# GLA's neighbour level as one more level in the burst of small products

## The chip, the cores and the metric

The kernel runs on one core of a Trainium2 chip. The metric is the device time of one execution in microseconds. Before the change it is 1476.96 us, the median of three runs between 1476.38 and 1477.36 us.

The engines are called as the profile calls them: PE is TensorE, DVE is VectorE, ACT is ScalarE, POOL is GpSimd, SP is SyncE, which here issues nearly all DMAs.

## The reference: what is computed

One layer of a hybrid decoder runs over 1024 prompt tokens and 8 single sample tokens of width 1024. Two branches share one input projection: gated linear attention (GLA, 4 heads, key width 128, value width 256) and RWKV-7 (16 heads of 64). A sigmoid gate merges them, then come the output projection and a layer norm. The change touches only GLA's attention inside a chunk. For one head it is, in the reference:

```python
b = jnp.cumsum(gi, axis=2)
diff = b[:, :, :, None, :] - b[:, :, None, :, :]
decay = jnp.exp(jnp.where(mask, diff, -jnp.inf))
A = jnp.einsum('bhid,bhjd,bhijd->bhij', qi, ki, decay)
o = jnp.einsum('bhij,bhjv->bhiv', A, vi) + jnp.einsum('bhid,bhdv->bhiv', qi * jnp.exp(b), S)
```

`A[i, j]` is the product of query i and key j over the 128 key dimensions, each dimension decayed by its own factors between token j and token i. All values are float32.

## The kernel before, in words

**Passes and blocks.** The 1024 tokens are done in two passes of 512 (the first with the 8 samples beside it). `blocks` sends the input projection through PE in blocks of 128 output columns; every product is done in three parts with operands split into a high and a low share (`wpart`, `xs`), accumulated in the PSUM banks `proj`. ACT and DVE move the results into row buffers (`row`, 33 of them). When the rows of a GLA head or of an RWKV pair are there, its own chain of work is started (`gla_head`, `pair`). After the second pass's projections come the up projections of both branches and the output projection, which are almost nothing but wide products on PE.

**What sets the order.** Each piece of work is a Python generator, a stream, that yields one operation after the other. `Order.run` is a list scheduler: it looks at the next operation of every stream, reckons with a table of costs (`price`) when it could start, subtracts the stream's priority, and writes down the earliest. Operations named `E` may go to DVE or POOL, those named `C` to ACT or DVE, whichever would end first by the reckoning. The result is one fixed order of instructions for each engine. A change in any stream therefore shifts the order of all of them. `together` makes one operation of a list of products, so that they stand on PE without anything between them.

**The GLA head.** It runs eight times: four heads, two passes, one after the other (`headed`). A head works on rows of 128 key dimensions (partitions) by 512 tokens: `qp_` holds the queries, `km_` the keys, `al` the decay of each token. Two chunks of 128 tokens are interleaved in a row (`paired`), the second backwards in time. The matrix A of a chunk is built by levels m = 1, 2, 4, ... 64 (`LEVELS`). At level m a chunk is cut into blocks of 2m tokens; the level gives the products of the queries of one half of each block with the keys of the other half. After each level the keys and queries of the halves are multiplied in place by the decay over their half (`E.tensor_mul(y, y, ...)`, two products and a small third for the next level's decays), so that plain products give decayed ones.

The levels are done in four ways before the change:

- *The diagonal* (token with itself, `d0`). DVE or POOL multiplies keys and queries element by element into a row (`u`), DVE transposes it in blocks of 32x32 (`STREAM_TRANSPOSE`), sums each block's rows (`TENSOR_REDUCE`, into the tile `pair`), and adds the four groups of 32 partitions with small sums. A masked copy (`copy_predicated`, mask `lev`) puts the sums on the diagonal of `AC`, a tile that holds the 32x32 blocks on A's diagonal.
- *Level 1*, the neighbours (`d1`), in the same way: a second element-by-element product, a second transpose and reduction, the second half of the same small sums, and a second masked copy, beside the diagonal. Only then come the decay products of level 1.
- *Levels 2 to 16* (`small`). For each, two copies on ACT or DVE put the level's keys and queries (128x256 each) side by side into a row (`kept`). At level 32 one `together`, the burst, multiplies 32 keys with 32 queries for each of the eight diagonal blocks and each level, into one PSUM bank `pl`; masked copies take from each result the places of its level into `AC`.
- *Level 32* goes in the same burst straight from the keys and queries; *level 64* has products of its own.

The rows `kept` of the four levels are the two spare rows `z` and `vk1` and two more that are fetched for it. The burst is `big<-row 128x32` in the profile: 5 x 8 products, each of which stands there as two records.

All operations go through one helper (L217), so the groups of the profile are told apart by their tiles and shapes.

## Time and profile before

| what | value |
|---|---|
| median of three runs | 1476.96 us |
| the profiled execution | 1478.35 us |
| its span, first to last instruction | 1476.5 us |
| mean granted clock of PE | 0.998 |
| busy: PE, DVE, ACT, POOL | 1446.6, 1163.0, 878.9, 108.8 us |
| HBM traffic over the span | 214 GB/s |

The profile's groups give busy time, the mean length of one in ns, and the idle time of the engine before them with what ended it. Matmuls are pipelined and their ends are modelled, so PE's busy share is not a share of its peak. Waits give the engine that waited, what ended the wait, and then the total, the number and the longest. In the chain, each step is followed back to what released it.

### The profile page before, as it was taken

The page shows a single profiled execution, that of the slowest core. Times are in us where ns is not written, and L with a number is a line of the kernel's source. Part 1 is how long each engine was busy: PE and PEld are TensorE (multiplying, and loading weights), DVE is VectorE, ACT ScalarE, POOL GpSimd, SP SyncE. Part 2 cuts the span into 40 slices and gives each one's busy share as a digit, 9 for nine tenths or more (in the row PEclk, how much of TensorE's full clock was granted, in tenths as well). Part 3 has the DMA queues.
Part 4 walks back from the last instruction along what each step waited for, and adds up shares of the span by engine and source line. Part 5 has one row for each costly group of instructions (what it writes and reads, how often), then busy time and mean ns, then how long its engine had stood idle before and what let it go on. Part 6 is the DMA issues. An engine that isn't in the chain of part 4 may idle for free.

```text
span 1476.5 us, 31483 instructions
## 1 busy us (share of the span) xinstructions
PE 1446.6 (98%) x11158; PEld 1258.8 (85%) x11158; DVE 1163.0 (79%) x3071; ACT 878.9 (60%) x2302; POOL 108.8 (7%) x205
## 2 busy tenths in 40 slices
PE   9999999999999999999999999999999999999997
PEld 6999989999999998787878777778787899988786
DVE  6697879987899777967998898888876876755665
ACT  5666767775776677655775564465546746643210
POOL 1001010100110001000110210020000000000000
PEclk9999999999999999999999999999999999999999
DMA  8877887669765878548646457656654768987432
GB/s 308 278 260 228 260 268 239 215 212 313 259 240 193 289 259 269 174 140 249 207 131 198 148 160 240 205 153 172 182 172 142 246 196 253 295 300 258 135 109 84
DMA packets 211258, 318.96 MB, mean 216 GB/s; under 512 B 91811, under 2 KB 107180, under 8 KB 211100
## 3 DMA queue, kind: packets, MB, share of 16 engines
q1 hardware_dynamic: 211100, 316.93, 67.1%
q8 instruction: 89, 1.46, 0.4%
q14 instruction: 69, 0.57, 0.1%
HBM read 197.19 MB, written 118.61 MB: 214 GB/s over the span
## 4 chain that ended last, share of the span: by engine, by line
PE 77%; DVE 14%; ACT 3%; DMA 2%; issue 2%; SPq 1%; POOL 0%; POOLq 0%; DVEq 0%; ACTq 0%
PE proj L217 48%; PE big L217 20%; DVE row L217 6%; PE pch L217 5%; PE pY L217 4%; ACT row L217 2%; DVE X L217 1%; DVE wide L217 1%; DVE Xt L217 1%; SPq L217 1%; DVE pair L217 1%; ACT L401 1%; DVE az L217 1%; DVE bk L217 1%; DVE ac L217 1%
## 5 line engine op out<-in xcount | busy, mean ns | idle before, releaser
L217 PE MATMUL proj<-xs,wpart 128*128 128x264 f32 (+2 forms) x5640 | 1022.8, 327 | 1.0 <-DVE row L217 0.8
L217 PEld LDWEIGHTS proj<-xs,wpart 128*128 128x128 f32 x5640 | 811.2, 189 | 82.1 <-issue 10.3
L217 DVE TENSOR_TENSOR row<-row 128x512 f32<-128x512 f32 (+8 forms) x327 | 173.1, 537 | 13.0 <-ACT row L217 6.6
L217 ACT CAST wpart<-wraw 128x512 fp32r<-128x512 f32 x210 | 129.6, 622 | 89.7 <-PE proj L217 36.3
L217 DVE TENSOR_TENSOR wpart<-wraw,wpart 128x512 fp32r<-128x512 f32 x198 | 137.2, 695 | 34.4 <-ACT wpart L217 32.0
L217 ACT ACTIVATE row<-row 128x512 f32<-128x512 f32 (+3 forms) x197 | 117.6, 606 | 13.0 <-DVE row L217 4.1
L217 PE MATMUL big<-xs,wpart 128*128 128x512 f32 (+2 forms) x576 | 102.9, 332 | 0.8 <-DVE xs L217 0.7
L217 DVE TENSOR_TENSOR Xt<-X,wide 128x60 f32<-128x60 f32 (+21 forms) x432 | 94.7, 219 | 9.4
L217 ACT ACTIVATE row<-proj,omu 128x256 f32<-128x256 f32 (+1 forms) x99 | 54.0, 546 | 77.7 <-PE proj L217 77.2
L217 POOL TENSOR_TENSOR row<-row 128x512 f32<-128x512 f32 (+7 forms) x58 | 60.2, 1043 | 536.7 <-DVE row L217 190.5
L217 DVE TENSOR_TENSOR X<-X,Xt 128x60 f32<-128x60 f32 (+21 forms) x432 | 91.8, 212 | 9.7
L217 PEld LDWEIGHTS big<-xs,wpart 128*128 128x128 f32 x576 | 87.0, 191 | 11.9 <-DVE xs L217 1.6
L217 DVE SCALAR_TENSOR_TENSOR wide<-pch,pc,s0p 64x64 f32<-64x64 f32 x208 | 58.8, 283 | 41.6 <-PE pch L217 35.6
L217 ACT COPY rh<-pch 128x128 f32<-128x128 f32 x104 | 27.5, 264 | 84.8 <-PE pch L217 83.8
L401 ACT ACT_TABLE_LOAD x60 | 77.0, 1283 | 1.0
L217 DVE SCALAR_TENSOR_TENSOR row<-proj,pv,row 128x255 f32<-128x255 f32 (+1 forms) x99 | 56.4, 570 | 23.5 <-ACT tail L217 12.3
L217 ACT COPY row<-big 128x128 f32<-128x128 f32 (+7 forms) x144 | 41.1, 308 | 51.5 <-PE big L217 43.2
L217 PE MATMUL big<-row 128*32 128x32 f32 (+4 forms) x944 | 67.3, 243 | 0.8 <-ACT row L217 0.8
L217 ACT COPY row<-wide 64x64 f32<-64x64 f32 x240 | 58.2, 242 | 5.8 <-DVE wide L217 1.8
L217 ACT CAST xs<-row 128x520 fp32r<-128x520 f32 (+1 forms) x64 | 38.4, 622 | 29.2 <-PE proj L217 10.3
L217 PEld LDWEIGHTS pch<-wide,gg 128*128 128x128 f32 x256 | 41.9, 188 | 14.5 <-PE proj L217 5.6
L217 PE MATMUL pch<-wide,gg 128*128 128x128 f32 x256 | 51.2, 281 | 2.9 <-DVE wide L217 1.8
(252 smaller groups left out, 2008.9 us busy)
## 6 DMA issues: line engine op xcount, KB each, us to landing
w<-wpart SPq DMA_DIRECT2D x146, 512.0 KB
wpart<-w SPq DMA_DIRECT2D x146, 512.0 KB
wraw<-w_in SPq DMA_DIRECT2D x146, 256.0 KB
wide<-LD SPq DMA_DIRECT2D x64, 128.0 KB
wraw<-w_up_gla SPq DMA_DIRECT2D x32, 256.0 KB
wraw<-w_up_rwkv SPq DMA_DIRECT2D x32, 256.0 KB
sg<-row SPq DMA_DIRECT2D x16, 260.0 KB
row<-sg SPq DMA_DIRECT2D x16, 260.0 KB
```

The costliest lines, as they stand in the source:

```text
L217: ways.append((eng, lambda call=call: call(out, *args, **kw), price(eng, name, out, args, ins)))
L401: self.nc.scalar.preload_act_table_set(self.table)
```

## The change

Level 1 becomes one of the levels of the burst. `small` is now 1, 2, 4, 8, 16. For level 1 the element-by-element product, the block transpose, the reduction and the second half of the small sums are gone, and so is the masked copy from `d1`. Instead two copies put level 1's keys and queries into a row, the burst has eight more products (48 instead of 40), and a masked copy takes the neighbours from PSUM as for the other levels. The diagonal stays as it was; its sums are now half as wide and partly done in place, so `pair` has two tiles of 16 columns in place of three of 32. Three row buffers are fetched for `kept` in place of two.

```diff
-    "pair": ([P, 2, HT // 32], 3), "nst": ([P, 2 * NCH], 2), "ac": ([P, HT // 4], 1),
+    "pair": ([P, HT // 32], 2), "nst": ([P, 2 * NCH], 2), "ac": ([P, HT // 4], 1),
...
-        r, r2, dd = yield from self.get("pair", 3)
+        r, dd = yield from self.get("pair", 2)
         yield E.tensor_mul(u.rearrange("p (a e q) -> p a q e", e=2, q=GC), self.paired(q), self.paired(k))
         yield E.tensor_mul(qp_, qp_, al[:, :HT])
         yield V.transpose(w, u)
-        yield V.tensor_reduce(r[:, 0], self.blocks32(w), mybir.AxisListType.X, ALU.add)
-        half, four, two = NGC // 2, (4, HT // 4), [(2 * GC, NGC // 2), (2, GC // 2)]
-        yield E.tensor_mul(self.strided(u, 0, *two, (GC + 1, 2)),
-                           self.strided(km_, 0, (2 * GC, half), (4, GC // 2), (3, 2)),
-                           self.strided(qp_, 2, (2 * GC, half), (4, GC // 2), (-1, 2)))
-        yield V.transpose(w, u)
-        yield V.tensor_reduce(r[:, 1], self.blocks32(w), mybir.AxisListType.X, ALU.add)
+        yield V.tensor_reduce(r, self.blocks32(w), mybir.AxisListType.X, ALU.add)
+        half = NGC // 2
         b = [slice(32 * i, 32 * i + 32) for i in range(4)]
         for i in (0, 2):
-            yield V.tensor_add(r2[b[i]], r[b[i]], r[b[i + 1]])
+            yield V.tensor_add(r[b[i]], r[b[i]], r[b[i + 1]])
         for i in range(4):
-            yield V.tensor_add(dd[b[i], :, 0:NGC], r2[b[0], :, i::4], r2[b[2], :, i::4])
-        d0, d1 = (dd[:, i, 0:NGC].rearrange("p (a e) -> p a e", e=2).unsqueeze(2) for i in range(2))
+            yield V.tensor_add(dd[b[i], 0:NGC], r[b[0], i::4], r[b[2], i::4])
+        d0 = dd[:, 0:NGC].rearrange("p (a e) -> p a e", e=2).unsqueeze(2)
...
-        yield V.copy_predicated(self.strided(AC, 2, (2 * B32, half), (4, B32 // 2), (-1, 2)),
-                                eye.rearrange("p (b e) -> p b e", e=2).unsqueeze(1).to_broadcast([P, half, B32 // 2, 2]),
-                                d1.to_broadcast([P, half, B32 // 2, 2]))
-        self.free(r, r2, dd)
-        kept = [z, vk1, *(yield from self.rows(2))]
+        self.free(r, dd)
+        kept = [z, vk1, *(yield from self.rows(3))]
         tot, pl = al[:, :HT], None
-        small, mms = [m for m in LEVELS if 1 < m < B32], []
+        small, mms = [m for m in LEVELS if m < B32], []
...
-                                            lev[:, lo + 1].rearrange("p (b e m) -> p b e m", e=2, m=y),
+                                            lev[:, lo].rearrange("p (b e m) -> p b e m", e=2, m=y),
```

The scheduler makes a new order of all engines from this. Three places of it follow.

DVE, the first head, between the diagonal's transpose and the first decay products (`pair` are the reductions and small sums, `X` belongs to an RWKV pair, `wpart<-wraw` is the low share of a weight). Before:

```order
L217 STREAM_TRANSPOSE row<-row 128x512
L217 TENSOR_REDUCE pair<-row 128x16
L217 TENSOR_TENSOR row<-row 128x2x64x2
L217 STREAM_TRANSPOSE row<-row 128x512
L217 TENSOR_REDUCE pair<-row 128x16
L217 TENSOR_TENSOR wpart<-wraw,wpart 128x512
L217 TENSOR_TENSOR pair<-pair 32x32 x2
L217 SCALAR_TENSOR_TENSOR X<-wide,X 128x31
L217 TENSOR_TENSOR pair<-pair 32x2x4
```

And with the change:

```order
L217 STREAM_TRANSPOSE row<-row 128x512
L217 TENSOR_REDUCE pair<-row 128x16
L217 TENSOR_TENSOR pair<-pair 32x16 x2
L217 TENSOR_TENSOR pair<-pair 32x4 x4
L217 COPY_PREDICATED ac<-lev,pair 128x128
L217 TENSOR_TENSOR wpart<-wraw,wpart 128x512
L217 TENSOR_TENSOR row<-row 128x128x2
L217 SCALAR_TENSOR_TENSOR X<-wide,X 128x31
L217 TENSOR_TENSOR row<-row 128x128x2
```

The second product, transpose and reduction are gone, the small sums have moved together, and the first decay products (`row<-row 128x128x2`) have moved up to the place where the small sums of the neighbours stood.

PE, the first head's burst, behind the same run of projection blocks. Before:

```order
L217 MATMUL proj<-xs,wpart 128x264 x24
L217 MATMUL proj<-xs,wpart 128x256 x24
L217 MATMUL proj<-xs,wpart 128x264 x17
L217 MATMUL big<-row 32x32 x40
L217 MATMUL proj<-xs,wpart 128x264 x7
```

And with the change:

```order
L217 MATMUL proj<-xs,wpart 128x264 x19
L217 MATMUL big<-row 32x32 x48
L217 MATMUL proj<-xs,wpart 128x264 x5
L217 MATMUL proj<-xs,wpart 128x256 x24
L217 MATMUL proj<-xs,wpart 128x264 x24
```

The burst stood 24 + 24 + 17 = 65 products behind that run and now stands 19 behind it, 46 earlier.

PE, the last head's burst, behind the product `big<-cons,Sp` that ends an RWKV pair. Before:

```order
L217 MATMUL proj<-xs,wpart 128x512 x6
L217 MATMUL big<-cons,Sp 64x128
L217 MATMUL proj<-xs,wpart 128x512 x29
L217 MATMUL big<-row 32x32 x40
L217 MATMUL proj<-xs,wpart 128x512 x5
```

And with the change:

```order
L217 MATMUL proj<-xs,wpart 128x512 x6
L217 MATMUL big<-cons,Sp 64x128
L217 MATMUL proj<-xs,wpart 128x512 x25
L217 MATMUL big<-row 32x32 x48
L217 MATMUL proj<-xs,wpart 128x512 x4
```

Here the burst has moved up by four products only.

## The prediction

> **What bounds the kernel now.** I read the first lines of the page and its chain of waits first, to see which engine sets the end.
>
> ```profile
> span 1476.5 us, 31483 instructions
> PE 1446.6 (98%) x11158; PEld 1258.8 (85%) x11158; DVE 1163.0 (79%) x3071; ACT 878.9 (60%) x2302; POOL 108.8 (7%) x205
> PE 77%; DVE 14%; ACT 3%; DMA 2%; issue 2%; SPq 1%; POOL 0%; POOLq 0%; DVEq 0%; ACTq 0%
> ```
>
> PE is busy for 98% of the span and stands on 77% of the chain. VectorE (DVE) stands on 14% of it and ScalarE (ACT) on 3%. So a microsecond taken from VectorE should be worth about a seventh of one at the end, and one given to PE nearly a whole one.
>
> The busy share hides something, though. I set the groups of the widest projection products against a row of the chain in order of time (start, length, what, count) from near the end, where PE does nothing else.
>
> ```profile
> L217 PE MATMUL proj<-xs,wpart 128*128 128x512 f32 x1872 | 503.3, 406 | 0.0
> L217 PE MATMUL pY<-xs,wpart 128*128 128x512 f32 x48 | 11.4, 394 | 0.0
> 1294.40 5.58 PE pY L217 x24
> ```
>
> Twenty-four products of the same width take 5.58 us there, 0.233 us each. Over the whole run such a product keeps PE "busy" for 503.3 / 1872 = 0.269 us. About 0.036 us of each, 67 us in all, is thus not work at full rate: short delays that lie under the modelled end of the product before, and switches between kinds of product. PE is the bound, but not a solid wall, and help can reach places that the list of idle times does not show.
>
> Next, where VectorE is dense. The view by stretches has, after the stretch, its length and then busy time and count for PE, PEld, DVE, ACT and POOL, and behind them the granted clock, the DMA share and GB/s:
>
> ```profile
> 200.00:300.00 100.00, 98.62 (x992) 95.51 (x993) 89.90 (x265) 76.00 (x217) 8.59 (x19) 1.00 0.70 234
> 700.00:800.00 100.00, 97.50 (x688) 79.53 (x687) 90.43 (x259) 69.44 (x179) 15.26 (x26) 1.00 0.61 183
> 1300.00:1476.50 176.50, 168.76 (x752) 135.26 (x751) 105.39 (x165) 46.10 (x101) 3.14 (x4) 0.99 0.52 174
> ```
>
> In two of the middle stretches VectorE is 90% busy: it is second in line there. In the last stretch (60%) only PE counts, and GLA's neighbour level has no part in it. Last, what PE openly waited for (us in total, times, longest):
>
> ```profile
> PE pch L217 <- DVE wide L217: 3.3, 8, 0.9
> PE big L217 <- DMA X<-XD: 2.1, 1, 2.1
> PE big L217 <- issue: 1.8, 3, 0.6
> PE big L217 <- DVE part L217: 1.7, 4, 0.7
> PE big L217 <- POOL XT L562: 1.7, 1, 1.7
> PE big L217 <- DVE S L217: 1.6, 2, 1.3
> PE big L217 <- DVE row L217: 1.3, 3, 0.8
> PE big L217 <- DVE l2p L217: 1.3, 2, 0.9
> PE big L217 <- DVE X L217: 1.3, 1, 1.3
> ```
>
> VectorE ended 3.3 + 1.7 + 1.6 + 1.3 + 1.3 + 1.3 = 10.5 us of these. That is the part that less work on VectorE can reach in plain sight.
>
> **What the change removes.** All of it happens once a head and pass, eight times. The rows, by group and, for the elementwise product, from the first head in the timeline:
>
> ```profile
> 75.26 0.63 DVE L217 TENSOR_TENSOR row<-row 128x256 f32<-128x256 f32 x1
> L217 DVE STREAM_TRANSPOSE row<-row 128x512 f32<-128x512 f32 x16 | 11.3, 708 | 0.2
> L217 DVE TENSOR_REDUCE pair<-row 128x16 f32<-128x512 f32 x16 | 10.9, 683 | 0.2
> L217 DVE TENSOR_TENSOR pair<-pair x48: 159/165/188, 78.0 to 1100.5; 32x8 f32<-32x8 f32 x32, 32x32 f32<-32x32 f32 x16
> L217 DVE COPY_PREDICATED ac<-lev,pair x16: 293/301/312, 81.2 to 1101.9; 128x128 f32<-128x128 uint8 x8, 128x64 f32<-128x64 uint8 x8
> L217 DVE COPY_PREDICATED ac<-lev,big x32: 292/300/307, 95.1 to 1113.7; 128x64 f32<-128x64 uint8 x32
> ```
>
> Half of the transposes go (8 x 0.708 = 5.7 us), half of the reductions (8 x 0.683 = 5.5 us), and the product: in the order seven of the eight stood on VectorE (7 x 0.63 = 4.4 us) and one on GpSimd. Together 15.6 us of VectorE. The six small sums a head stay and only shrink (32x32 becomes 32x16, 32x8 becomes 32x4). Their time hardly hangs on the size (159 to 188 ns over both shapes), so I take nothing; at most 48 x 0.03 = 1.4 us more is saved, and a loss has no reason. The masked copy of the neighbours is replaced by one of equal shape that reads PSUM: 300 ns against 301, no difference.
>
> **What it adds.** Two copies of 128x256 a head, eight products of 32x32 a head, and one more row buffer held (three instead of two) until the burst.
>
> ```profile
> L217 ACT COPY row<-row 128x256 f32<-128x256 f32 x47 | 19.1, 431 | 17.4 <-DVE row L217 16.9 <-POOL row L217 0.2
> L217 DVE COPY row<-row 128x256 f32<-128x256 f32 x25 | 6.9, 287 | 0.0
> 93.65 0.91 PE L217 MATMUL big<-row 128*32 128x32 f32 x80
> 94.48 0.75 PE L217 MATMUL proj<-xs,wpart 128*128 128x264 f32 x4
> L217 PEld LDWEIGHTS big<-row 128*32 128x32 f32 x704 | 7.9, 110 | 3.9 <-issue 2.4 <-PE big L217 0.4
> ```
>
> A product of f32 stands as two records: the 40 of a burst are 80. From the burst's start to the next product of PE are 94.48 - 93.65 = 0.83 us, 10.4 ns a record. Eight more products are 16 records, 0.166 us a head, 1.33 us over the run. They join a burst that is there anyway, so no further switch is paid. As it is PE's own time, I put all of it on the path.
>
> [...]
>
> Of the copies, the built order gives 17 more to ScalarE (17 x 0.431 = 7.3 us) and takes one from VectorE (0.3 us). The order is made by a planner that weighs all work anew, so other steps move too:
>
> ```profile
> L217 ACT COPY wide<-pch 64x64 f32<-64x64 f32 x160 | 33.0, 206 | 22.9 <-PE pch L217 18.7
> L217 DVE COPY wide<-pch 64x64 f32<-64x64 f32 x96 | 21.3, 221 | 19.2 <-PE pch L217 14.0 <-ACT s0p L217 2.6 <-ACT row L217 0.2
> L401 ACT ACT_TABLE_LOAD x60 | 77.0, 1283 | 1.0
> ```
>
> Thirty-two of the small copies of the RWKV chain go from VectorE to ScalarE (-7.1 us there, +6.6 us here), and the order has two table loads fewer (-2.6 us). VectorE: -15.6 - 0.3 - 7.1 = -23.0 us. ScalarE: +7.3 + 6.6 - 2.6 = +11.3 us.
>
> **The sum.** VectorE at its share of the chain: -23.0 x 0.14 = -3.2 us. ScalarE: +11.3 x 0.03 = +0.3 us. PE: +1.33 us. Together -1.5 us. Against the profiled span of 1476.5 us this is 1475.0 us; I carry the same difference to the median of the runs, 1476.96 us, and get 1475.4 us. (The profiled execution as a whole took 1478.35 us, 1.4 us over that median, so its rows need no scaling.)
>
> The bounds of VectorE's part: it is worth nothing if PE never waits for it, and then the result is 1476.96 + 1.3 + 0.3 = 1478.6 us. It is worth 10.5 us if every open wait that VectorE ended goes: 1476.96 - 10.5 + 1.6 = 1468.1 us. More is possible only out of the 67 us of hidden delay. The third row buffer I cost at nothing, since projection blocks already under way cover it. If that cover is gone, a block starts late by about one evacuation, 0.473 us, eight times 3.8 us:
>
> ```profile
> L217 ACT ACTIVATE row<-proj,omu 128x256 f32<-128x256 f32 x33 | 15.6, 473 | 28.8 <-PE proj L217 28.7
> ACT row L217 <- PE proj L217: 116.4, 105, 4.8
> ```
>
> **The rivals.** *Relief worth much more.* VectorE really sets the pace in the 90% stretches. For it: PE loses 36 ns on each wide product there. Against it: PE's open waits on VectorE are 0.9 us at most in the RWKV chain. If half of the 10.5 us goes and as much again of hidden delay, that is -10.5 + 1.6: about 1468 us, and half of it alone gives 1473.3 us. I name 1471.
>
> *Slower: the burst becomes a wait.* Before, the neighbour sums and the first level's decay products stood on VectorE one behind the other. Now the decay products, which overwrite keys and queries in place, must first wait for two copies on ScalarE; and ScalarE's queue stops behind evacuations that wait for PE (the row above: 116.4 us in 105 waits, 1.1 us each). The planner also puts the first burst 46 projection products earlier in PE's order, as shown with the change. Behind the two copies in ScalarE's queue stand the next evacuation and the next weight cast, and behind the burst in PE's queue the projections that these feed. If the copies are late, PE stands still in front of the burst with nothing behind it that may pass. One such wait of 1.1 us a head costs 8.9 us: 1475.4 + 8.9 = 1484.3 us. It decides the sign from (1.5 + 3.0) / 8 = 0.56 us a burst on. Against it: before, the weight loads of all bursts waited 3.9 us together, of which 0.4 us for PE and none, by the row, for ScalarE or VectorE.
>
> *The relief is absorbed.* Shorter heads only end earlier and nobody waits for them. The last burst speaks for it: it stands at nearly the same place among the projections as before, also shown with the change. Then only PE's own addition counts: about 1478 us.
>
> **How the numbers follow.** A measurement of this kernel can tell about 0.2%, 3 us, from no change. The sum as worked out (1475.4 us; its own range 1472 to 1478.6) has a chance of 0.40, the larger relief 0.25, the late burst 0.23, the absorbed relief 0.12. Faster by over 3 us: a quarter of the first case, nearly all of the second: 0.35. Slower by over 3 us: most of the third, a little of the first and the last: 0.25. Within 3 us: 0.40. The eightfold-in-ten range takes in the lower bound worked out above and most of the late burst: 1467 to 1483 us.
>
> **What would show it.** The burst: 96 records in about 1.0 us before the next product. VectorE near 1140 us busy, ScalarE near 890. Transposes and reductions into `pair` at 8 each. Open waits of PE that VectorE ended below 10 us; with the absorbed relief they stay and the weight loads of projections slow by as much as the bursts grow. With the late burst, PE or its weight loads show idle time before the 128x32 products ended by ScalarE, over 4 us in all. The prediction is wrong in kind if PE's busy time grows by more than 2 us with no such wait, or if the time moves by more than 8 us and the moved work lies outside the heads: then the planner's new order, not the removed work, made the difference.

## The result, and the profile after

The changed kernel takes 1487.36 us (median of 6 runs, 1485.48 to 1492.16), the kernel before in the same comparison 1477.16 us (6 runs, 1475.17 to 1478.82). The ratio is 1.0073, 95% interval 1.0062 to 1.0084: slower by 10.2 us, where 1.5 us less was forecast, and above the forecast's range, which ended at 1483 us. The profiled execution took 1486.16 us with a span of 1484.4 us, against 1478.35 and 1476.5 us before, so the traces show 7.9 us of the 10.2. Among the runs further below, two single executions, one of each of two kernels, took 4.9 ms and are left out of all medians.

The first lines of the page after, and the shares of its chain of waits:

```profile
span 1484.4 us, 31676 instructions
PE 1449.1 (98%) x11286; PEld 1261.7 (85%) x11286; DVE 1144.7 (77%) x3028; ACT 887.8 (60%) x2339; POOL 104.3 (7%) x201
PE 35%; DVE 4%; DMA 2%; issue 0%; ACT 0%; SPq 0%; POOL 0%; POOLq 0%; DVEq 0%
```

VectorE is busy 18.3 us less and ScalarE 8.9 us more, as intended, and PE 2.5 us more. The span less PE's busy time, which is how long PE had nothing in hand, went from 1476.5 - 1446.6 = 29.9 us to 1484.4 - 1449.1 = 35.3 us. That is 5.4 of the 7.9 us. (The chain could be followed back only through 41% of the span this time, so its shares say nothing here.)

The groups of the work that was removed, added and moved, and from the timeline the first head's burst with the first product behind it:

```profile
L217 DVE STREAM_TRANSPOSE row<-row 128x512 f32<-128x512 f32 x8 | 5.6, 705 | 0.0
L217 DVE TENSOR_REDUCE pair<-row 128x16 f32<-128x512 f32 x8 | 5.5, 683 | 0.0
L217 ACT COPY row<-row 128x256 f32<-128x256 f32 x64 | 26.1, 429 | 20.9 <-DVE row L217 19.2 <-POOL row L217 0.7
L217 ACT COPY wide<-pch 64x64 f32<-64x64 f32 x192 | 39.7, 207 | 21.1 <-PE pch L217 14.9
L217 PE MATMUL big<-row 128*32 128x32 f32 x768 | 9.0, 199 | 0.4 <-DVE Xt L217 0.3
L217 PEld LDWEIGHTS big<-row 128*32 128x32 f32 x832 | 9.3, 110 | 4.0 <-issue 2.3 <-DVE Xt L217 0.4 <-DVE row L217 0.2
87.44 1.03 PE L217 MATMUL big<-row 128*32 128x32 f32 x96
88.40 9.32 PE L217 MATMUL proj<-xs,wpart 128*128 128x264 f32 x76
```

The burst's group before, for comparison:

```profile
L217 PE MATMUL big<-row 128*32 128x32 f32 x640 | 7.5, 199 | 0.0
```

Each is where the prediction put it: transposes and reductions at 8 each, 64 copies of 128x256 on ScalarE, and a burst whose group is 9.0 - 7.5 = 1.5 us longer over the run. The first burst takes 88.40 - 87.44 = 0.96 us for its 96 records, where 0.83 us for 80 was measured before. Before the burst's products PE stood idle for 0.4 us in all, and nothing there was ended by ScalarE. The burst did not become a wait.

Then the view by stretches (columns as in the prediction). Two stretches before that it did not show:

```profile
100.00:200.00 100.00, 97.40 (x896) 91.69 (x896) 78.61 (x212) 69.79 (x193) 10.88 (x20) 1.00 0.76 238
1200.00:1300.00 100.00, 97.99 (x791) 92.19 (x790) 66.20 (x139) 57.32 (x123) 0.00 (x0) 0.98 0.82 261
```

After:

```profile
100.00:200.00 100.00, 96.02 (x863) 89.25 (x862) 77.03 (x200) 69.99 (x190) 11.69 (x23) 0.98 0.75 238
200.00:300.00 100.00, 96.96 (x951) 93.41 (x950) 84.63 (x239) 74.25 (x215) 5.59 (x12) 1.00 0.67 217
700.00:800.00 100.00, 97.91 (x634) 78.63 (x633) 78.32 (x203) 66.22 (x170) 10.25 (x19) 1.00 0.60 171
1200.00:1300.00 100.00, 95.45 (x796) 91.29 (x795) 64.15 (x136) 57.87 (x123) 0.00 (x0) 0.97 0.75 241
```

VectorE has come down from 90% to 85% and 78% in the dense stretches, and PE does not gain there to speak of: 98.6 has become 97.0 and 97.5 has become 97.9. Against this PE loses 1.4 us between 100 and 200 us and 2.5 us between 1200 and 1300 us, and the granted clock is lower in both. The second of these is behind the last head: GLA's neighbour level has no work in it at all (its last masked copy out of a burst starts at 1119 us). So part of the loss lies where nothing was changed but the order.

What PE openly waited for, after (the largest rows that VectorE ended, and those of ScalarE from 1.0 us on; the rest is left out):

```profile
PE pch L217 <- DVE wide L217: 6.1, 8, 1.6
PE big L217 <- DVE l2p L217: 2.6, 2, 1.3
PE big L217 <- DVE part L217: 1.9, 2, 1.0
PE pch L217 <- ACT wide L217: 1.7, 3, 0.6
PE big L217 <- ACT row L217: 1.6, 2, 1.2
PE pch L217 <- ACT rh L217: 1.5, 1, 1.5
PE big L217 <- ACT bk L217: 1.3, 1, 1.3
PE big L217 <- ACT wide L217: 1.0, 1, 1.0
PE pch L217 <- ACT row L217: 1.0, 1, 1.0
```

ScalarE ended 1.7 + 1.6 + 1.5 + 1.3 + 1.0 + 1.0 = 8.1 us of PE's waits. Before, no row of ScalarE in this view was over 1.0 us. All rows of ScalarE together have grown from 1.7 to 8.6 us, all of VectorE from 12.9 to 14.8 us. And the RWKV chain's wait for VectorE, which has less to do now, has grown from 3.3 to 6.1 us. Both engines are late in other places than before, in the RWKV chain and the projections it interleaves with, not at the work that was replaced.

### The profile page after: what moved, and what is told of

Its sections match the earlier page's. It is cut to its first block, busy times and chain, and to the rows that moved or that the text cites. A ratio compares the mean times of both kernels' runs of the same rounds, so it can differ in the third digit from the quotient of the medians.

```text
span 1484.4 us, 31676 instructions
## 1 busy us (share of the span) xinstructions
PE 1449.1 (98%) x11286; PEld 1261.7 (85%) x11286; DVE 1144.7 (77%) x3028; ACT 887.8 (60%) x2339; POOL 104.3 (7%) x201
## 5 line engine op out<-in xcount | busy, mean ns | idle before, releaser
L217 DVE TENSOR_TENSOR row<-row 128x512 f32<-128x512 f32 (+10 forms) x327 | 172.4, 535 | 13.8 <-ACT row L217 5.2
L217 ACT ACTIVATE row<-row 128x512 f32<-128x512 f32 (+5 forms) x197 | 118.1, 608 | 17.4 <-DVE row L217 7.2
L217 PE MATMUL big<-xs,wpart 128*128 128x256 f32 (+2 forms) x576 | 100.9, 330 | 0.0
L217 POOL TENSOR_TENSOR row<-row 128x512 f32<-128x512 f32 (+6 forms) x50 | 54.7, 1097 | 615.1 <-DVE row L217 218.7
L217 DVE SCALAR_TENSOR_TENSOR row<-proj,pv,row 128x255 f32<-128x255 f32 (+1 forms) x99 | 56.5, 570 | 25.9 <-ACT tail L217 18.3
L217 ACT COPY row<-big 128x128 f32<-128x128 f32 (+6 forms) x135 | 38.8, 316 | 39.0 <-PE big L217 29.4
L217 PE MATMUL pch<-wide,bk 128*128 128x128 f32 x256 | 50.6, 279 | 3.4 <-DVE wide L217 1.7
```

What stands on the lines that cost most here:

```text
L217: ways.append((eng, lambda call=call: call(out, *args, **kw), price(eng, name, out, args, ins)))
```

## The experiments

**First: the work or the order?** Theory *work*: the moved work itself costs the time (a busier PE, copies on ScalarE). Theory *order*: the planner's new order for everything else costs it. The first three kernels keep the instruction order of the kernel before to the letter. The planner sees and prices the old steps, but another instruction is issued in a step's place, or none (the helper `emits` exchanges what a step issues, `plus` adds to it).

The change's work, with its two copies on ScalarE; the third row buffer is one of its own (`nb`):

```diff
+        nb_ = yield from self.get("nb")
+        first = [self.A.copy(nbs[:, y]..., x) for y, x in enumerate(nsrc)]
-        yield E.tensor_mul(self.strided(u, 0, *two, (GC + 1, 2)), ...)
-        yield V.transpose(w, u)
-        yield V.tensor_reduce(r[:, 1], self.blocks32(w), ...)
+        yield emits(E.tensor_mul(self.strided(u, 0, *two, (GC + 1, 2)), ...))
+        yield emits(V.transpose(w, u), first[0])
+        yield emits(V.tensor_reduce(r[:, 1], self.blocks32(w), ...), first[1])
...
-                yield together(mms)
+                yield plus(together(mms), *more)
```

> The change's own work, put into the order of the kernel before: every other instruction of every engine stands where it stood. The second product, transpose and reduction are not issued; at the places of the latter two the two copies go to ScalarE; the burst has 48 products; the third row is a buffer of its own. Theory 'order' (the loss of 10 us comes from the planner's new order of everything else): no loss here, 1474 to 1479 us, by my own sum 1475.4 + 0.3. Theory 'work' (the copies on ScalarE make the burst late, or PE's addition is dearer than 1.3 us): 1484 us or more, with waits of PE ahead of the burst.

Measured: 1476.88 us, ratio 0.9994 (0.9978 to 1.0011).

The same with the copies on VectorE, where the transpose and the reduction stood (the diff is against the kernel just shown):

```diff
-        first = [self.A.copy(nbs[:, y]..., x) for y, x in enumerate(nsrc)]
+        first = [self.V.copy(nbs[:, y]..., x) for y, x in enumerate(nsrc)]
```

> As the run with the copies on ScalarE, but both copies stand on VectorE in the very places of the transpose and the reduction (0.287 us in place of 0.7 each). Theory 'order': 1473 to 1478 us, no slower than the one with ScalarE. Theory 'work', if it is ScalarE's queue that makes the burst late: this one is free of the loss (1477 us or less) while the one with ScalarE is not; if it is PE's addition: both lose alike.

Measured: 1476.39 us, ratio 0.9991 (0.9977 to 1.0005).

The neighbour level taken out and nothing put in its place:

```diff
+        yield emits(E.tensor_mul(self.strided(u, 0, *two, (GC + 1, 2)), ...))
+        yield emits(V.transpose(w, u))
+        yield emits(V.tensor_reduce(r[:, 1], self.blocks32(w), ...))
```

> The order of the kernel before with the neighbour level left out: second product, transpose, reduction, half of the small sums and the second masked copy are not issued and nothing takes their place, so the attention lacks the products of neighbouring tokens. It prices VectorE's relief alone (-15.6 us of its work and 8 masked copies of 0.3 us more, some 18 us). By the chain's share as I predicted: 18 x 0.14 = 2.5 us less, 1474.6 us. If the relief is absorbed: 1476.5 to 1477.5 us. If VectorE sets the pace: 1468 us or less.

Measured: 1473.55 us, ratio 0.9977 (0.9968 to 0.9987).

And the reverse, the order of the changed kernel with the old work issued on VectorE in it, no copies and no further products:

```diff
-        yield V.tensor_reduce(r, self.blocks32(w), ...)
+        yield plus(V.tensor_reduce(r[:, 0], self.blocks32(w), ...),
+                   V.tensor_mul(self.strided(u, 0, *two, (GC + 1, 2)), ...),
+                   V.transpose(w, u),
+                   V.tensor_reduce(r[:, 1], self.blocks32(w), ...))
...
-                yield together(mms)
+                yield emits(together(mms), *mms[8:])
```

> The reverse: the order of the changed kernel, but in it the old work. Second product, transpose, reduction and wide small sums are issued on VectorE behind the first reduction, the two copies of level 1 and its eight products are not issued. Result as before. Theory 'order': the loss stays, 1486 to 1492 us (VectorE's 18 us are back, PE's 1.3 us gone). Theory 'work': the loss goes, 1475 to 1479 us.

Measured: 1505.11 us, ratio 1.0198 (1.0176 to 1.0221).

In the old order the new work costs nothing that can be measured, on either engine. The lost time therefore belongs to the order, and theory *work* falls. In the new order even the old work is slow, slower than the new. This fits, but 1505 us is more than either theory had named (1486 to 1492, or 1475 to 1479 us), and there is a limit: work that is issued in places planned for other work is not what a planner would have made of it, so the 17.7 us between the last kernel and the changed one are no clean price of anything. The first two kernels also differ from the change in a buffer: their third row is one of its own and is not fetched from the 33 rows. What that fetching costs, a kernel in the third group of experiments answers.

The third kernel prices the relief: VectorE's busy time fell from 1163.0 to 1149.6 us, by 13.4 us, and the time by about 3.4 us, a quarter of it. (The instructions left out come to the expected 18 us, but VectorE's instructions overlap in the records: before, their durations add up to 1266.4 us where its busy time is 1163.0. Of 18 us the 3.4 are a fifth.) Putting the new work in gives 3.3 us (copies on ScalarE) or 2.8 us (on VectorE) of that back. So the exchange of work is worth 0.4 to 0.9 us by the medians, not distinguishable from nothing.

**Second: is the new order late in one place or in many?** The trace after has clusters of new waits in two places, with the granted clock lower at both than at the same places before (0.89 against 1.00 and 0.77 against 0.89, over the windows of 15 us shown in the fourth group of experiments). Near 193 us a weight cast on ScalarE waits 2.65 us for its DMA, the copy `bk` stands behind it, and PE waits 1.34 us for that copy. (The kernel before waits there too, 2.1 us for the load of `X` in the prediction's list, but at full clock.) Near 1232 us five products of the RWKV chain follow one another in PE's queue with no projection between them. The timeline there, after:

```profile
1231.37 0.49 PE L217 MATMUL pch<-wide,bk 128*128 128x128 f32 x2 [0.55 <-ACT wide L217]
1232.72 0.46 PE L217 MATMUL pch<-wide,gg 128*128 128x128 f32 x2 [0.87 <-DVE wide L217]
1234.71 0.80 PE L217 MATMUL pch<-rh,XT 128*128 128x128 f32 x2 [1.53 <-ACT rh L217]
1236.02 0.79 PE L217 MATMUL pch<-wide,bk 128*128 128x128 f32 x2 [0.51 <-ACT wide L217]
```

Each waits for what ScalarE or VectorE makes of the one before: 0.55 + 0.87 + 1.53 + 0.51 = 3.5 us in 5 us. The first kernel issues the casts that are in the way a few steps later (numbers are steps of the planner):

```diff
+MOVE = {2211: 2217, 12902: 12919, 12906: 12919, 12907: 12919, 12908: 12919, 12909: 12919, 12911: 12919}
...
+            if self.nth in MOVE:
+                self.late.append((MOVE[self.nth], op.fn))
+            else:
+                op.fn()
```

> The changed kernel with its order altered at two places alone, and nothing added or taken away. (1) Near 190 us the weight cast on ScalarE that waited 2.65 us for its DMA goes behind the two copies (a row and bk) that stood behind it; (2) near 1232 us three casts of xs on ScalarE, the first of which waits for the load of o_rwkv, and the three subtractions on VectorE that follow them go behind one step of the RWKV chain (rh, s0p, wide) that stood behind them. Theory 'two places' (PE's waits there and the half-clock stretches that follow, 3.4 us at 196 us and 6.8 us at 1234 us, make most of the loss): 1478 to 1483 us, 4 to 9 us less than the changed kernel, and at most one half-clock stretch left before the end. Rival 'spread' (the loss lies in many small delays all along): 1485 us or more.

Measured: 1487.63 us, ratio 1.0077 (1.0062 to 1.0092), against 1.0073 unmended. Its trace, in the two places and near 740 us:

```profile
190.00:205.00 15.00, 14.24 (x139) 12.92 (x136) 10.21 (x25) 9.67 (x29) 2.62 (x8) 1.00 0.94 327
738.00:748.00 10.00, 9.01 (x39) 7.56 (x40) 8.16 (x31) 3.04 (x12) 0.00 (x0) 0.83 0.48 156
1236.00:1246.00 10.00, 8.16 (x43) 7.67 (x43) 4.18 (x9) 6.08 (x18) 0.00 (x0) 0.66 0.54 182
```

The first place is mended (14.24 us of 15 busy, at full clock). The second is not, and the clock now falls near 740 us. Over the run PE had nothing in hand for 36.1 us, no less than the 35.3 us before the mending. The second kernel fills the gaps near 1232 us with products that nobody reads:

```diff
+FILL = {12895: 6, 12903: 8, 12910: 14, 12917: 6}
...
+            if self.nth in FILL:
+                spare = self.make["pY"]()
+                for _ in range(FILL[self.nth]):
+                    self.nc.tensor.matmul(spare[:, :P], self.onesr, self.headsr, start=True, stop=True)
```

> The changed kernel with its order, and with 34 products of 128x128 that nobody reads, put into PE's queue between the five products of the RWKV chain near 1232 us, where PE waited 0.5 to 1.5 us each time. They do not shorten the chain, they only keep PE busy while it waits. If the half-clock stretch comes from PE being idle and costs what it seems (6.8 us at half rate, 3.4 us of work): no such stretch there, and 1483 to 1485 us, 2 to 4 us less than the changed kernel. If the stretch is only a mark of the waits and costs nothing by itself: no gain, 1487 to 1490 us.

Measured: 1486.08 us (three executions), ratio 1.0072 (1.0052 to 1.0092). The profiled execution took 1481.73 us and shows the place filled, at full clock:

```profile
1230.00:1245.00 15.00, 14.76 (x123) 14.38 (x123) 8.96 (x21) 10.18 (x31) 0.00 (x0) 1.00 0.60 194
```

By the ratios nothing was gained (1.0072 against 1.0073), and the median lies between what the two theories named. The profiled execution is the fastest of the three. It has no half-clock stretch near 196 us either, where nothing was changed, and a mean clock of 0.999; the other two (1486.08 and 1487.09 us) had 0.996. So the stretches come and go between executions of one kernel. "Two places" finds no support: mending either one gave nothing back, and new waits came up elsewhere. It is not refuted, since the first kernel mended only the first place, the second only the second, and none both. Whether the five chained products alone are worth something stays unclear.

**Third: is this order late by rule or by chance?** If the change led the planner astray by rule (a busier ScalarE, say), any order it makes for the changed kernel should be slow. If it is chance, other orders of both kernels should scatter alike. The planner's constants were nudged, one at a time, in both kernels, with the computation left as it is: what PE's inputs are given as a margin, what a change of partition group costs, and what a change of tile shape costs.

```diff
-SPARE = 0.4
+SPARE = 0.42
```

> The kernel before with one of the planner's constants moved by a twentieth (the time it adds to a result of another engine that PE reads, 0.4 to 0.42 us). No instruction is added or taken away except where the planner chooses another engine; the order changes everywhere. Theory 'chance' (an order is a draw, and the change drew a bad one): the time moves by several us either way, 1470 to 1490. Theory 'systematic' (the old planner costs give good orders for the old work, the new work gives bad ones): within 3 us of 1477.

> The changed kernel with the same constant at 0.42 us. Theory 'chance': a new draw from the same spread as the kernel before, 1470 to 1490, as likely below 1487 as not, with a mean of the draws near that of the draws of before. Theory 'systematic': 1484 us or more, and above its partner of before by 7 us or more.

```diff
-HOLD = 0.11
+HOLD = 0.12
```

> The kernel before with the planner's charge for a change of partition group on VectorE and ScalarE at 0.12 in place of 0.11 us. Same expectations as for the other moved constant: 'chance' 1470 to 1490, 'systematic' within 3 us of 1477.

> The changed kernel with that charge at 0.12 us. 'Chance': 1470 to 1490, mean of the draws as for before. 'Systematic': 1484 us or more, 7 us above its partner.

```diff
-SWITCH = 0.09
+SWITCH = 0.1
```

> The same for the kernel before. 'Chance': 1470 to 1500, with half-clock stretches in number about (time - 1474) / 3. 'Systematic': within 3 us of 1477.

> A further draw of an order for the changed kernel: the planner's charge for a change of tile shape on PE at 0.10 in place of 0.09 us. 'Chance': 1470 to 1500, with half-clock stretches before the end in number about (time - 1474) / 3. 'Systematic': 1484 us or more.

Medians in us, with the ratio to the kernel before and its interval:

| order made with | the old work | the new work |
|---|---|---|
| constants as they were | 1477.16 | 1487.36, 1.0073 (1.0062 to 1.0084) |
| SPARE 0.42 | 1481.45, 1.0029 (1.0015 to 1.0042) | 1476.05, 0.9992 (0.9982 to 1.0003) |
| HOLD 0.12 | 1500.22, 1.0169 (1.0131 to 1.0207) | 1480.52, 1.0026 (1.0014 to 1.0039) |
| SWITCH 0.1 | 1482.21, 1.0044 (1.0027 to 1.0061) | 1485.92 (two executions), 1.0067 (1.0046 to 1.0089) |
| mean of the four | 1485.3 | 1482.5 |

With a margin of 0.42 instead of 0.40 us the changed kernel is the faster of the two by 5 us. Four orders of each kernel spread over 23 and 11 us, and their means do not tell the kernels apart. "By rule" falls, since two of the four orders of the changed kernel lie clearly under the 1484 us that it named. One order of the kernel before (1500.22 us) lies outside the range of "chance" too. The kernel with SPARE at 0.42 fetches its third row from the pool and is level with the kernel before, so the third row is no reason for a loss by itself. The order that the kernel before had is the best of the four drawn for it, and the change gave that up for one of the slower ones of its own four. Whether the planner's constants had once been chosen because they gave the old work a good order is not on record; it would make that order better than an average draw.

The number of half-clock stretches that was expected with SWITCH at 0.1, (time - 1474) / 3, came out roughly: counted in units of 3.41 us the two traces have 5 (new work, 1488.28 us, 4.8 expected) and 5 (old work, 1484.64 us, 3.5 expected). This estimate does not hold for all kernels: the new order with the old work has 6 at 1504.10 us, where it gives 10.

**Fourth: what does a standstill of PE cost?** The pages of all these kernels have one thing in common: the longer the span, the longer (with a few exceptions) PE had nothing in hand. Here with the span of the profiled execution, and with the time that the trace's record of the clock shows at half rate before PE's last work, in us:

| kernel | span | PE with nothing in hand | at half clock before the end |
|---|---|---|---|
| old order, new work on VectorE | 1470.1 | 26.7 | 0 |
| old order, level left out | 1472.1 | 28.7 | 0 |
| new work, SPARE 0.42 | 1474.2 | 30.8 | 0 |
| old order, new work on ScalarE | 1476.1 | 30.7 | 3.4 |
| before | 1476.5 | 29.9 | 3.4 |
| new work, HOLD 0.12 | 1478.7 | 33.8 | 0 |
| after, gaps near 1232 us filled | 1480.0 | 30.8 | 0 |
| old work, SPARE 0.42 | 1481.0 | 32.9 | 6.8 |
| old work, SWITCH 0.1 | 1482.9 | 35.4 | 17.1 |
| after | 1484.4 | 35.3 | 10.2 |
| new work, SWITCH 0.1 | 1486.4 | 34.3 | 17.1 |
| after, two places mended | 1487.3 | 36.1 | 10.2 |
| old work, HOLD 0.12 | 1496.6 | 43.9 | 27.3 |
| new order, old work | 1502.2 | 45.1 | 20.5 |

Each row is one execution, and executions of one kernel scatter (those of the first row from 1471.90 to 1478.40 us, and its trace is the fastest of them), so only the trend counts. From the first row to the last the standstill grows by 18.4 us and the span by 32.1 us. So something comes on top of the length of the waits. The clock had a candidate. In windows of 15 us around the two places, before:

```profile
190.00:205.00 15.00, 12.88 (x131) 11.69 (x130) 8.08 (x19) 8.85 (x27) 1.11 (x6) 1.00 0.92 291
1228.00:1243.00 15.00, 13.79 (x96) 12.93 (x95) 8.76 (x21) 9.34 (x26) 0.00 (x0) 0.89 0.74 237
```

After:

```profile
190.00:205.00 15.00, 12.62 (x103) 10.92 (x103) 7.99 (x18) 8.74 (x27) 2.62 (x8) 0.89 0.76 272
1230.00:1245.00 15.00, 11.54 (x71) 10.70 (x71) 8.54 (x18) 9.68 (x28) 0.00 (x0) 0.77 0.53 179
```

Within the half-clock stretch before (1231.46 to 1234.87 us, granted clock 0.50) the products `big<-xs,wpart` of 128x264 start 220 ns apart at the median, at full clock 122 ns. By that I estimate the loss as the missing share of the clock times the length: a mean clock of 0.89 over 15 us is 1.65 us of work at full rate, and 0.77 is 3.45 us. The trace's record of the clock has these as stretches at half rate of 3.41 us, or twice that: 3.41 us before (near 1232 us), 3.41 us (near 196 us) and 6.83 us (near 1234 us) after. Four kernels measured the price. In the order of before, at up to eight places, PE gets two small products, and the second waits until GpSimd has filled a tile so many times (0.53 us each in the runs below, 1.05 us for two in the first of them):

```diff
+            if self.nth in GAP:
+                spare = self.make["pY"]()
+                for n in (GAP[self.nth], 0):
+                    self.nc.tensor.matmul(spare[:, :P], self.still[:, :P], self.still[:, :P], start=True, stop=True)
+                    for _ in range(n):
+                        self.nc.gpsimd.memset(self.still, 0.0)
```

> The kernel before, with two extra 128x128 products behind one another at eight places of PE's order (near 80, 172, 240, 310, 885, 895, 911 and 1037 us), nothing between them: the base for the three runs below. All theories: sixteen products more, 1477.2 us plus 1 to 4 us, no more half-clock stretches than the kernel before has (one of 3.41 us before PE's last work).

> As the base, but at each of the eight places GpSimd fills a tile twice (0.53 us each) between the two products, so PE must stand still for 1.1 to 1.3 us, 9 to 10 us in all. Theory 'length' (a standstill of PE costs its length, and the others catch up meanwhile): base + 5 to 10 us, no new half-clock stretch. Theory 'clock' (a standstill also costs a stretch of 3.41 us at half the clock, about 1.7 us of lost work): the same if 1.2 us is too short to set one off, else up to base + 10 + 8 x 1.7 = base + 24 us, with 3.41 us or a multiple behind most gaps.

> As the base, but at four of the places (80, 240, 885 and 1037 us) four fills each, so four standstills of 2.1 to 2.3 us, about 9 us in all. Theory 'length': the same time as the eight short ones within 1 us or so, base + 5 to 9 us. Theory 'clock': base + 9 + 4 x 1.7 = base + 16 us, with a half-clock stretch behind each of the four.

> As the base, but at two of the places (240 and 895 us) eight fills each, so two standstills of 4.2 to 4.4 us, about 9 us in all. Theory 'length': again base + 5 to 9 us. Theory 'clock': base + 9 + 2 x 1.7 = base + 12 us or more, with a half-clock stretch at both places and nowhere else.

Measured: the base 1477.96 us, ratio 1.0002 (0.9993 to 1.0011). Eight short standstills 1489.43 us, 1.0072 (1.0056 to 1.0089), 11.5 us over the base. Four middle ones 1494.65 us, 1.0108 (1.0085 to 1.0132), 16.7 us over it. Two long ones 1491.72 us, 1.0084 (1.0063 to 1.0105), 13.8 us over it.

PE's waits in the kernel with eight short ones, and then by the clock the first and the last of the eight places, with a stretch between them:

```profile
PE pY L408 <- POOL still L410: 6.3, 5, 1.3
PE pY L408 <- POOL row L218: 3.8, 3, 1.3
```

```profile
80.00:85.00 5.00, 3.78 (x31) 3.78 (x32) 3.67 (x16) 1.96 (x8) 1.10 (x3) 1.00 0.77 293
772.00:780.00 8.00, 6.66 (x51) 5.51 (x44) 7.00 (x14) 4.66 (x10) 0.00 (x0) 0.79 0.35 140
1048.80:1053.80 5.00, 3.73 (x17) 3.11 (x18) 2.51 (x11) 1.11 (x3) 1.11 (x3) 1.00 0.36 117
```

Eight waits of 1.3 us, 10.1 us together, cost 11.5 us by the medians: all of their length, and nothing is caught up later. At none of the eight places did the clock drop. It dropped near 774 us, behind the wait of 1.3 us for VectorE's `S` that every one of these kernels has (in the waits of before, in the prediction). The base has that wait at the same place of its order, and there the clock stayed up:

```profile
766.00:774.00 8.00, 6.39 (x60) 4.88 (x58) 7.83 (x15) 5.27 (x11) 0.63 (x1) 1.00 0.46 185
```

With four middle ones, PE's waits and then the clock:

```profile
PE pY L408 <- POOL row L218: 7.3, 3, 2.5
PE pY L408 <- POOL still L410: 2.4, 1, 2.4
PE pY L218 <- issue: 2.0, 1, 2.0
```

```profile
80.30:87.00 6.70, 4.31 (x36) 4.30 (x36) 4.02 (x17) 2.49 (x9) 2.15 (x5) 1.00 0.60 222
452.00:460.00 8.00, 5.98 (x59) 5.83 (x59) 4.09 (x17) 2.21 (x7) 0.00 (x0) 0.79 0.19 69
894.10:902.00 7.90, 5.44 (x19) 4.35 (x19) 3.65 (x13) 0.39 (x1) 2.16 (x5) 0.78 0.86 311
```

Of the four standstills of 2.4 us one (894 us) is followed by a half-clock stretch, and so is a wait of 2.0 us near 452 us, which I had not put there. The sum for the profiled execution: 9.7 + 2.0 us of waits, and 0.21 x 8.0 + 0.22 x 7.9 = 3.4 us by the clock, 15.1 us, against 1493.0 - 1475.3 = 17.7 us between the spans. With two long ones (4.7 and 4.8 us) the clock reads:

```profile
239.20:248.00 8.80, 4.09 (x21) 4.09 (x22) 2.68 (x5) 1.99 (x8) 4.39 (x10) 0.81 0.31 62
453.90:463.00 9.10, 6.87 (x53) 6.75 (x53) 3.98 (x15) 2.19 (x7) 0.00 (x0) 0.62 0.27 74
907.60:917.00 9.40, 4.62 (x15) 3.69 (x15) 3.34 (x13) 1.11 (x3) 4.25 (x9) 0.82 0.32 109
```

Both standstills (near 239 and 908 us) are followed by a stretch of 3.41 us at half rate, worth 0.19 x 8.8 = 1.7 us each. Two more were not expected: 6.83 us that begin within a wait of 2.2 us near 454 us, and 3.41 us near 780 us, behind the wait for `S`. Theory *length* wanted the same time from all three and falls (11.5 against 16.7 us, of which 2.0 us is the wait near 452 us that was not put there). Theory *clock* came near in size (16 and 12 us expected, 16.7 and 13.8 measured), in part by luck: not every standstill of 2.4 us set off a stretch, and stretches and a wait at other places made up for it. The last section has what the windows of the traces show. What made PE wait at 452 us when everything before it had moved stays open. In both traces a 16 KB packet of the queue that the page lists for instructions (q8) was under way there that took 2.19 and 2.23 us, where the median is 1.0 us, and PE went on 1.39 and 1.40 us after its end. That PE waited for its instructions there is not shown: other packets as long were followed by no such wait, and no run tests it.

No kernel beat both: the old order with the new work on VectorE (1476.39 us) and the new work planned with SPARE at 0.42 (1476.05 us) are level with the kernel before.

## Why the prediction was wrong

**The step that failed** is the sentence "The order is made by a planner that weighs all work anew, so other steps move too", together with the sum that follows: it has no term for what a new order costs. I priced the new order by counting what it moved between engines (32 small copies, two table loads) and multiplied the counts by shares of the chain. An order has a price that no count shows: how often PE comes to a product whose input is not there yet. With the old order held, the exchange of work gave 1476.88 and 1476.39 us, level with the kernel before; with the new order it gave 1487.36 us. The runs give the price of an order a spread of 11 to 23 us over four orders of one kernel, against a net 1.5 us for everything that the sum held. The closing remark named it ("then the planner's new order, not the removed work, made the difference"), but as a sign that I was wrong, not as a case with a chance, and it was the case that came true.

**The terms of the sum, one by one.** *The work on the engines*: VectorE -18.3 us busy against -23.0, ScalarE +8.9 against +11.3, the burst +1.5 against +1.33. These were right in kind. *VectorE's share of 0.14*: the run without the level gave 3.4 us for 18 us of VectorE's instructions, counted as the sum counts them, a share of 0.19 (0.25 of the 13.4 us of busy time). It was too small, but the relief is real. *ScalarE's share of 0.03*: in the old order the copies on ScalarE and the larger burst together gave 3.3 us back, more than my 1.6 us. The two errors largely cancel, which is luck: the exchange of work alone is worth 0.4 to 0.9 us, and the sum said 1.5. *The third row buffer*, put at nothing, is borne out by the kernel with SPARE at 0.42, which fetches it and is level with the kernel before. *The switches between kinds of product* have no number of their own in the prediction: in the trace before, after a projection product of 128x512 the next of its kind starts 233 ns later at the median, the first of a burst (`big<-row` 128x32, four cases) 322 ns later.

**The price of the burst.** The prediction's 1.33 us came from the first burst before, at 10.4 ns a record for 128 added records. From a burst's start to the next product the traces have 0.83 to 0.91 us before, 6.9 us over the eight bursts, and 0.96 to 1.50 us after, 8.9 us. That is 2.0 us more, 0.34 us of it a wait for VectorE's `Xt` inside the fifth burst. So the price was 1.7 to 2.0 us: the prediction had taken the first burst, one of the shortest, and came out too low, though a record of the first burst still took 10.0 ns after (0.96 us for 96).

**The rivals.** *The burst becomes a wait* came nearest in time (1484.3 us) and is wrong in mechanism: PE stood idle for 0.4 us before the products of the burst, none of it ended by ScalarE, where over 4 us were named as its mark. It is right only in that late ScalarE copies now hold up PE (8.1 us), in other places. *Relief worth much more* and *relief absorbed* were both questions about the old order. The run without the level answers them: about a fifth of the relief arrives.

**The marks.** I expected VectorE's part of PE's open waits to fall below 10 us, since VectorE has less to do. All its rows together went from 12.9 to 14.8 us, the three largest alone are 10.6 us. Less work on an engine did not make it less late, because an order decides when that work comes.

**Where the 7.9 us between the traces went.** PE had nothing in hand for 5.4 us more and was busy for 2.5 us more, and the two are the 7.9. The burst (1.5 us of busy time) and the two further half-clock stretches, worth 3.45 us by the windows above (1.65 + 3.45 - 1.65), would make the busy part 4.95 us. Why only 2.5 us of it shows is not settled: a product that runs at half rate may partly fill a wait that would have come after it, which no run tests. Why the planner's order comes out late with these constants and not with the next ones is not settled either. That it is late in many places is argued from PE's waits and from the two mendings that gained nothing, and not shown.

## What to carry to other kernels

Where a planner or scheduler makes the order from modelled costs, any edit draws a new order, and its luck can outweigh the edit: here 1477 to 1500 us for the same work. Price the edit with the order held, and judge it against several orders of both kernels, not one of each; forecast with the spread of such orders as the range. Here, on an engine that is busy for 98%, eight waits of 10.1 us together cost 11.5 us, their full length, and nothing was caught up, so the sum of its idle time is the first number to compare between two traces. The second is the time at half clock, which came on top in stretches of 3.41 us, about 1.7 us of work each, also where two waits of 0.61 and 1.35 us lay some 3 us apart.

## What the hardware showed that was not expected

A standstill of PE can cost more than its length: with four middle ones 11.7 us of waits went with a span longer by 17.7 us. Behind both standstills of 4.7 and 4.8 us, one of four of 2.4 us, and none of eight of 1.3 us, the granted clock fell to 0.5 for 3.41 us, some 1.7 us of work. And one and the same wait of 1.3 us near 770 us was followed by such a stretch in one kernel and not in another. The stretches before PE's last work have one length or twice that: 3.413 us in the kernel before, 3.413 and 6.827 us in the changed one. With the eight short standstills a wait of 1.3 us (near 773 us) was followed by one, with the four middle ones a wait of 2.0 us (near 452 us) and one of 2.5 us (near 894 us), while others of the same lengths were not.

The traces show what goes with it. In each of the 12 traces with more than one half-clock stretch (the one behind PE's last work is counted) they start whole multiples of 3.413 us apart: with the two long standstills at 243.84, 455.47, 779.74 and 912.86 us, which are 62, 95 and 39 steps, and in the trace after at 196.18, 1233.83 and 1479.59 us, which are 304 and 72. So I divided each trace into windows of that length on its own grid (the other six on the start of their last stretch) and took how long PE had nothing in hand within each. Near 770 us the kernel with sixteen more products and no standstill, and the one with eight short ones, both have the same two waits, 0.61 us and about 1.35 us, some 3 us apart. In the first the window holds only the longer wait, in the second that one and most of the other (stretch, length, busy time and count of PE, PEld, DVE, ACT and POOL, clock):

```profile
766.60:770.01 3.41, 2.06 (x19) 1.39 (x14) 3.34 (x9) 1.96 (x4) 0.03 (x1) 1.00 0.93 378
770.31:773.72 3.41, 1.62 (x22) 1.06 (x23) 3.37 (x7) 1.92 (x5) 1.61 (x2) 1.00 0.95 334
```

PE had nothing in hand for 1.35 us of the first window and the clock stayed up; for 1.79 us of the second, and the half-clock stretch starts where it ends (773.72 us). I counted the windows of all 18 traces, from the first one at full clock to about 10 us before the last stretch, without the windows right behind one at half clock. All 18 windows in which PE had nothing in hand for 1.85 us or more were followed by a stretch, 12 of the 27 with 1.45 to 1.85 us, and one of the 7609 with less (before, near 1231 us, with 1.04 us). The four standstills of 2.4 us agree: three were divided by the grid and left 1.5 to 1.7 us in one window, and the one near 894 us left 2.3 us. So in these 18 traces the fall goes with PE's time without work summed over all waits of one window: from 1.85 us on, 0.54 of a window, it always came. What decides between 1.45 and 1.85 us stays open, and what makes the clock fall at all no run shows.
